# Retention and pooling trunk on one core: PSUM as one pool of eight named banks, GpSimd's first loads held back, the input's first pieces over ScalarE's queue

## Chip, core and metric

One of the eight cores of a Trainium2 chip runs the kernel. The metric is the device time of one launch in microseconds (us); a lower time is better. TensorE is PE, VectorE is DVE, ScalarE is ACT, GpSimd is POOL and SyncE is SP in the rows of the profile.

## What is computed

Two layers over 256 tokens of 2048 numbers in float32, each with a norm before it and a plain residual add, and a last norm.

```
h = x
h = h + (group_norm(retention(rope(q), rope(k), v)) * silu(z)) @ ret_w_out    # q,k,v,z = rms_norm(h) @ ret_w_in, 8 heads
h = h + ((mix @ pool_w_grp + pool_b_grp) * pool_scale * silu(z)) @ pool_w_out # u,z = rms_norm(h) @ pool_w_in
out = rms_norm(h, final_norm)                                                 # mix = windowed mean of u, minus u
```

The weights are 236 units of 128 x 2048 float32 numbers (1024 KB each), plus the first four of `ret_w_in`, which come in pieces. Nearly all the arithmetic is products of these weights with 256 columns of activations.

## The kernel before

**Exactness.** Products run in the fast float32 form of TensorE, which keeps fewer bits of an operand. So each operand is split in two: `hi` is a rounded copy (a CAST on ScalarE, line 91) and `lo` is what is left (a subtraction on VectorE, line 92). A product is then hi x hi, hi x lo and lo x hi. For every weight unit SyncE loads `raw` (line 103, three buffers), ScalarE and VectorE split it in two halves `w` (five buffers), and TensorE multiplies.

**Stages.** (1) The startup (lines 188 to 245): nine products of ones (`cold`), then the input `xin` and the first four units arrive in pieces, each is split, and TensorE accumulates four results `accs`. GpSimd loads the identity `idt`, the rotation table `rp` and two masks `mk` at once. (2) Eight heads of retention (lines 249 to 353): q, k, v and gate products, scores, normalisation. Products that keep the weights stationary are written to `acc` by `stationary` (lines 122 and 123), those of v to `accv` (lines 302 to 304). (3) The way out, `way_out` with `ret_out` (lines 387 to 479): two passes, each of 12 plain units ("C") and 4 mixed units ("S", in which sums of blocks save products); all eight PSUM banks hold running sums `p1`, `p5`, `p6`, `p7`, `c11`, `c12`, `c21`, `c22` (line 363). When the sums of a half are ready, `turn` transposes the new stream on TensorE into `turned` (line 510) and splits it into `hs2`. (4) Pooling (lines 551 to 598): four groups of 8 + 8 units and 4 units of group weights, again by `stationary` into `acc`. (5) `way_out` with `pool_out`, with the last norm in it, and the output.

**Order.** The program text gives an order, and a scheduler that plays the program against its own timing model moves instructions on each engine's queue; each engine then runs its queue strictly in order. A tile may be written when its buffer is free, that is when the last reader of the tile that held it before is done.

**PSUM.** A partition has eight banks of 512 float32 numbers. Stages 1 and 2, and again stage 4, open two pools: three buffers for `acc`, five for the rest (`banks`, lines 80 to 86). Stages 3 and 5 each open a pool of their own with eight tags (lines 492 and 639). The pools of one stage are closed before those of the next are opened on the same memory.

The lines that the change touches: 78 to 86 (`banks`), 138, 188, 196, 197, 241, 256, 272, 292, 320, 341, 557, 578 and 587 (where a bank is taken), 358 (`Sum`), 387 and 399 (`way_out`), 204 (the input's pieces), 223 to 226 (GpSimd's loads), 491 to 520 and 638 to 645 (opening and closing).

Of the kernel before, what the change touches and what calls it, by code (L numbers as in the profile page):

```python
# [7 lines left out]
F32 = mybir.dt.float32  # L8
# [5 lines left out]
P = 128  # L14
D = 2048
S = 256
# [15 lines left out]
FIRST = (20, 16)  # L32

# [12 lines left out]
def kernel(  # L46
# [25 lines left out]
    nc = tc.nc  # L72
# [61 lines left out]
    def column_sums(sums):  # L134

        sp = ev.tile([P, 2, S], F32R, tag="sp", name="sp", bufs=1)
        split(sp[:, 0], sp[:, 1], sums)
        tot = psum[1].tile([P, 512], F32, tag="ret", name="tot")
# [45 lines left out]


    with banks("first"), tc.tile_pool(name="rt", bufs=1) as rt:

        cold = psum[1].tile([P, 512], F32, tag="ret", name="cold")
# [7 lines left out]
        accs = [psum[0].tile([P, 512], F32, tag="acc", name="acc") for _ in range(3)]  # L196
        accs.append(psum[1].tile([P, 512], F32, tag="ret", name="acc"))
# [43 lines left out]
        rst = psum[1].tile([P, 512], F32, tag="ret", name="rst")  # L241
# [7 lines left out]
        for h in range(NH):  # L249
# [3 lines left out]
            for c in range(4 if h else 0):  # L253
                blocks = blocks_of(weights(ret_in[unit]))
                unit += 1
                acc = psum[0].tile([P, 512], F32, tag="acc", name="acc")
                stationary(acc, blocks, hs)
                joined(qk[:, c], acc)
# [13 lines left out]
            sc = psum[1].tile([P, 2, S], F32, tag="ret", name="sc")  # L272
# [19 lines left out]
            accv = [psum[0].tile([P, 512], F32, tag="acc", name="accv") for _ in range(2)]  # L292
# [25 lines left out]
            for c in range(4):  # L318
                cs = slice(c * P, (c + 1) * P)
                po = psum[1].tile([P, 512], F32, tag="ret", name="po")  # L320
# [17 lines left out]
            for c in range(4):  # L338
                blocks = blocks_of(weights(ret_in[unit]))
                unit += 1  # L340
                acc = psum[0].tile([P, 512], F32, tag="acc", name="acc")
# [13 lines left out]
    class Sum:  # L355


        def __init__(self, pool, name, n):
            self.tile, self.n, self.done = pool.tile([P, 512], F32, tag=name, name=name), n, 0
# [27 lines left out]
    def way_out(A, src, first, forms, tmp, pool, work, order, y, after, ends=False):  # L387
# [8 lines left out]
        for p in range(2):  # L396
            plain = len(CLASSIC) // 2 * 12
            sums = {}
            for name in order:
                n = 0 if name == "c22" else 3 * NS  # L400
                sums[name] = Sum(pool, name, n + (plain if name[0] == "c" else 0))
# [79 lines left out]
    with tc.tile_pool(name="pl", bufs=1) as pl:  # L481
# [9 lines left out]
        with (  # L491
            tc.tile_pool(name="way1", bufs=1, space=bass.MemoryType.PSUM) as way,
            tc.tile_pool(name="work1", bufs=1) as work,
        ):
# [4 lines left out]
            def turn(t, c):  # L499
# [5 lines left out]
                for i in range(2):  # L505
                    turned = way.tile([P, 512], F32, tag=(("p1", "p5"), ("p6", "p7"))[c % 2][i], name="turned")
# [10 lines left out]
            order = ("p1", "p5", "p6", "p7", "c11", "c21", "c12", "c22")  # L517
            way_out(os, ret_out, FIRST[0], forms, tmp, way, work, order, stream, turn)
        second = ctx.enter_context(ExitStack())
        second.enter_context(banks("second"))  # L520
# [30 lines left out]
        for g, win in enumerate(WINDOWS):  # L551
# [3 lines left out]
            for c in range(GT):  # L555
                blocks = blocks_of(weights(pool_in[2 * GT * g + c]))
                acc = psum[0].tile([P, 512], F32, tag="acc", name="acc")
# [18 lines left out]
            for c in range(GT):  # L576
                blocks = blocks_of(weights(pool_in[2 * GT * g + GT + c]))
                acc = psum[0].tile([P, 512], F32, tag="acc", name="acc")
# [4 lines left out]
            for c in range(GT // 2):  # L583
                halves = weights(pool_grp[GT // 2 * g + c])
                for i in range(2):
                    e = GT * g + 2 * c + i
                    acc = psum[0].tile([P, 512], F32, tag="acc", name="acc")
# [50 lines left out]
        with (  # L638
            tc.tile_pool(name="way2", bufs=1, space=bass.MemoryType.PSUM) as way,
            tc.tile_pool(name="work2", bufs=1) as work,  # L640
        ):
            tmp = act.tile([P, 4 * S + 2 * P + 512], F32, tag="hs", name="tmp")
            forms = pl.tile([P, NS, 4, 2, P], F32R, tag="ms", name="forms")
            order = ("p1", "p5", "p6", "c11", "c21", "c12", "c22", "p7")
            way_out(gs, pool_out, FIRST[1], forms, tmp, way, work, order, stream, norm, True)

# [110 lines left out]
```

## Time and profile before

| | |
|---|---|
| median of 3 runs | 1393.86 us (1393.78 to 1394.25) |
| the profiled execution | 1391.64 us |
| its span | 1389.5 us |
| TensorE busy | 1364.1 us (98%) |
| VectorE, ScalarE, GpSimd busy | 1060.9 us (76%), 719.7 us (52%), 25.4 us (2%) |
| mean DMA rate | 189 GB/s |

The span is what the profiler saw between the first and the last instruction; the execution's own time lies 2.1 us above it. Matmuls are pipelined, so a row of TensorE shows each one longer than the step from one to the next. The granted clock of TensorE is given as a share of full speed: 1.00 is 2.4 GHz, 0.50 is 1.2 GHz.

### The profile page before, as it was taken

Reading aid. Unit: us, or ns where it says so; the run is one execution under the profiler, and the core shown is the slowest. Engines: PE = TensorE matmul, PEld = TensorE weight load, DVE = VectorE, ACT = ScalarE, POOL = GpSimd, SP = SyncE. Lnnn points to the kernel's source line nnn. Section 1 sums busy time; section 2 is a strip of 40 time slices with the busy share of each in tenths; the row PEclk is TensorE's granted clock in tenths of the full one; section 3 lists DMA queues with packets and bytes.
Section 4 is the critical chain, followed back from the end, with each engine's and each line's share of the span. In section 5 each row is a group of like instructions: output and inputs, shape, how many; then the busy total and the mean of one; then the engine's idle time right before and its main releaser. Section 6 shows DMA issues by size and latency. Waiting matters only on the chain.

```text
span 1389.5 us, 18380 instructions
## 1 busy us (share of the span) xinstructions
PE 1364.1 (98%) x7176; PEld 1171.6 (84%) x7176; DVE 1060.9 (76%) x1545; ACT 719.7 (52%) x1027; POOL 25.4 (2%) x33
## 2 busy tenths in 40 slices
PE   8999999999999999999998999999999999899997
PEld 7888888888888888888887888888888888788885
DVE  6886868686868686898777867876886896868676
ACT  6455545455545454555454455455545545545443
POOL 0000000000000000000000000000000000000102
PEclk8999999999999999999999999999999999999999
DMA  8545454545555545475555555555555555446552
GB/s 298 209 161 197 172 191 177 190 179 188 182 187 180 184 173 190 153 261 196 182 189 180 195 199 182 185 199 195 183 188 191 198 185 185 179 164 230 182 210 93
DMA packets 39493, 262.66 MB, mean 189 GB/s; under 512 B 4512, under 2 KB 4896, under 8 KB 9072
## 3 DMA queue, kind: packets, MB, share of 16 engines
q1 hardware_dynamic: 37872, 255.93, 52.0%
q0 software_dynamic: 1536, 5.57, 1.1%
q8 instruction: 56, 0.92, 0.3%
q14 instruction: 29, 0.24, 0.0%
HBM read 259.39 MB, written 2.10 MB: 188 GB/s over the span
## 4 chain that ended last, share of the span: by engine, by line
PE 96%; DVE 2%; ACT 1%; issue 1%; DMA 1%; SPq 0%; DVEq 0%; ACTq 0%
PE acc L122 37%; PE c L363 21%; PE acc L123 19%; PE accv L302 4%; PE accv L304 4%; PE accv L303 4%; PE p L363 3%; PE po L322 1%; DVE w L92 1%; DMA xin<-in_xT 1%; PE po L324 1%; PE sc L276 0%; DVE hs L97 0%; PE sc L281 0%; ACT w L91 0%
## 5 line engine op out<-in xcount | busy, mean ns | idle before, releaser
L92 DVE TENSOR_TENSOR w<-raw,w 128x1024 fp32r<-128x1024 f32 x472 | 568.1, 1209 | 168.0 <-ACT w L91 160.0
L122 PE MATMUL acc<-hs,w 128*128 128x512 f32 x1984 | 692.4, 392 | 3.5 <-DVE rs_t L161 3.5
L91 ACT CAST w<-raw 128x1024 fp32r<-128x1024 f32 x472 | 486.9, 1038 | 305.0 <-PE acc L123 130.7
L123 PE MATMUL acc<-hs,w 128*128 128x256 f32 x1984 | 556.1, 280 | 0.0
L122 PEld LDWEIGHTS acc<-hs,w 128*128 128x128 f32 x1984 | 372.0, 187 | 84.7 <-issue 3.7
L123 PEld LDWEIGHTS acc<-hs,w 128*128 128x128 f32 x1984 | 375.5, 189 | 1.0
L363 PE MATMUL c<-w,gs 128*128 128x512 f32 x624 | 149.3, 394 | 4.6 <-DVE m L592 4.6
L131 ACT COPY hl<-acc 128x256 f32<-128x256 f32 x128 | 47.9, 374 | 199.5 <-PE acc L123 197.0
L363 PE MATMUL c<-w,os 128*128 128x512 f32 x624 | 149.3, 391 | 0.9 <-DVE gz L132 0.9
L363 PEld LDWEIGHTS c<-w,gs 128*128 128x128 f32 x624 | 118.7, 190 | 30.6 <-issue 4.9
L363 PEld LDWEIGHTS c<-w,os 128*128 128x128 f32 x624 | 116.6, 188 | 26.1 <-DVE gz L132 1.2
L302 PE MATMUL accv<-w,hs 128*128 128x512 f32 x256 | 99.8, 390 | 1.2 <-DVE qk L132 1.2
L303 PE MATMUL accv<-w,hs 128*128 128x512 f32 x256 | 99.8, 390 | 0.0
L304 PE MATMUL accv<-w,hs 128*128 128x512 f32 x256 | 99.7, 390 | 0.0
L122 PE MATMUL acc<-ms,w 128*128 128x512 f32 x256 | 90.6, 397 | 0.0
L123 PE MATMUL acc<-ms,w 128*128 128x256 f32 x256 | 72.0, 281 | 0.0
L91 ACT CAST w<-s 128x1024 fp32r<-128x1024 f32 x32 | 33.6, 1050 | 52.0 <-PE c L363 43.9
L122 PEld LDWEIGHTS acc<-ms,w 128*128 128x128 f32 x256 | 48.1, 188 | 11.8
L92 DVE TENSOR_TENSOR w<-s,w 128x1024 fp32r<-128x1024 f32 x32 | 39.2, 1224 | 24.4 <-ACT w L91 24.4
L302 PEld LDWEIGHTS accv<-w,hs 128*128 128x128 f32 x256 | 48.1, 188 | 11.1 <-DVE qk L132 1.5
L304 PEld LDWEIGHTS accv<-w,hs 128*128 128x128 f32 x256 | 48.0, 188 | 10.1
L303 PEld LDWEIGHTS accv<-w,hs 128*128 128x128 f32 x256 | 48.1, 188 | 9.7
(159 smaller groups left out, 1052.7 us busy)
## 6 DMA issues: line engine op xcount, KB each, us to landing
raw<-in_ret_in SPq DMA_DIRECT2D x92, 1024.0 KB, 4.9
raw<-in_pool_in SPq DMA_DIRECT2D x64, 1024.0 KB, 4.9
raw<-in_ret_out SPq DMA_DIRECT2D x32, 1024.0 KB, 4.9
raw<-in_pool_out SPq DMA_DIRECT2D x32, 1024.0 KB, 4.9
raw<-in_pool_grp SPq DMA_DIRECT2D x16, 1024.0 KB, 4.9
xin<-in_ret_in SPq DMA_DIRECT2D x7, 512.0 KB, 8.5
xn<-in_xN POOLq DMA_DIRECT2D x4, 512.0 KB, 6.9
out<-xn SPq DMA_DIRECT2D x8, 256.0 KB, 2.3
```

Of the source, the lines that this page charges most:

```text
L91: nc.scalar.copy(hi, src)
L92: nc.vector.tensor_tensor(out=lo, in0=src, in1=hi.bitcast(F32), op=ALU.subtract)
L122: nc.tensor.matmul(acc, hi, moving[:, k], start=(k == 0), stop=False)
L123: nc.tensor.matmul(acc[:, :S], lo, moving[:, k, 0], start=False, stop=(k == n - 1))
L131: nc.scalar.copy(t, acc[:, S:])
L302: nc.tensor.matmul(accv[t], hs[:, k, 0, ts], hi[:, ws], start=(k == 0), stop=False)
L303: nc.tensor.matmul(accv[t], hs[:, k, 0, ts], lo[:, ws], start=False, stop=False)
L304: nc.tensor.matmul(accv[t], hs[:, k, 1, ts], hi[:, ws], start=False, stop=(k == KT - 1))
L322: nc.tensor.matmul(po[:, :S], vs[:, 0, p, cs], ss[:, q, :S], start=(n == 0), stop=(n == 2))
L324: nc.tensor.matmul(po[:, S:], vs[:, 1, p, cs], ss[:, :, S:], start=(p == 0), stop=(p == 1))
L363: nc.tensor.matmul(self.tile, a, w, start=(self.done == 0), stop=(self.done == self.n - 1))
```

## The change

All PSUM tiles come from one pool that stays open for the whole program and has eight tags, `b0` to `b7`, one buffer each. `ring("acc")` walks through banks 0 to 2, `ring("ret")` through banks 3 to 7, and both go on counting through the whole program; the sums of `way_out` have fixed banks by their place in `SUMS`, and `turned` takes banks 0, 1 or 2, 7. Besides, a one-element copy on GpSimd that reads `hs[:, 11, 1]` stands ahead of GpSimd's loads, and the first three pieces of the input are issued by ScalarE in place of SyncE. Cut to its core (every other place that took a tile from `psum[0]` or `psum[1]` now calls `ring("acc", ...)` or `ring("ret", ...)` in the same way):

```diff
+SUMS = ("p1", "p5", "p6", "c11", "c21", "c12", "c22", "p7")
...
-    psum = []
-
-    @contextmanager
-    def banks(name):
-
-        with tc.tile_pool(name=f"{name}_acc", bufs=3, space=bass.MemoryType.PSUM) as acc:
-            with tc.tile_pool(name=f"{name}_ret", bufs=5, space=bass.MemoryType.PSUM) as rest:
-                psum[:] = acc, rest
-                yield
+    psum = ctx.enter_context(tc.tile_pool(name="psum", bufs=1, space=bass.MemoryType.PSUM))
+    turns = {"acc": 0, "ret": 0}
+
+    def bank(i, name):
+        return psum.tile([P, 512], F32, tag=f"b{i}", name=name)
+
+    def ring(kind, name):
+
+        start, n = (0, 3) if kind == "acc" else (3, 5)
+        turns[kind] += 1
+        return bank(start + (turns[kind] - 1) % n, name)
...
-                nc.sync.dma_start(out=xin[:, k : k + n], in_=xT[:, k : k + n])
+                queue = nc.scalar if u == 0 else nc.sync
+                queue.dma_start(out=xin[:, k : k + n], in_=xT[:, k : k + n])
                 nc.sync.dma_start(out=raw[:, ws], in_=ret_in[u][:, ws])
...
+        late = rt.tile([P, 1], F32, name="late")
+        tc.keep_in_program_order(nc.gpsimd.tensor_copy(out=late, in_=hs[:, 11, 1, :1].bitcast(F32)))
         idt = const.tile([P, P], F32, name="idt")
         tc.keep_in_program_order(nc.gpsimd.dma_start(out=idt, in_=ident))
...
-            self.tile, self.n, self.done = pool.tile([P, 512], F32, tag=name, name=name), n, 0
+            self.tile, self.n, self.done = bank(i, name), n, 0
...
-                    turned = way.tile([P, 512], F32, tag=(("p1", "p5"), ("p6", "p7"))[c % 2][i], name="turned")
+                    turned = bank(((0, 1), (2, 7))[c % 2][i], "turned")
...
-        second.enter_context(banks("second"))
```

The scheduler makes other queues of the new program. Three places follow. The first is TensorE where pooling (stage 4) begins; `acc` is the result of one weight unit, `turned` a transposed block of the stream, `hs2` the split stream, `c22` a running sum of the stage before. Before:

```order
L363 MATMUL c22_5642<-w_6195,os_357 128x512 x6
L510 MATMUL turned_6228<-idt_303,xn_4987 128x128
L510 MATMUL turned_6237<-idt_303,xn_4987 128x128
L510 MATMUL turned_6228<-idt_303,xn_4987 128x128 x3
L510 MATMUL turned_6237<-idt_303,xn_4987 128x128 x3
L122 MATMUL acc_6280<-hs2_4997,w_6274 128x512
L123 MATMUL acc_6280<-hs2_4997,w_6274 128x256
```

Now, from the last of the running sum to the last transposes:

```order
L370 MATMUL c22_5635<-w_6189,os_356 128x512 x6
L125 MATMUL acc_6267<-hs2_4991,w_6261 128x512
L126 MATMUL acc_6267<-hs2_4991,w_6261 128x256
L125 MATMUL acc_6267<-hs2_4991,w_6261 128x512
L126 MATMUL acc_6267<-hs2_4991,w_6261 128x256
```

```order
L126 MATMUL acc_6267<-hs2_4991,w_6264 128x256
L514 MATMUL turned_6222<-idt_302,xn_4984 128x128 x3
L514 MATMUL turned_6231<-idt_302,xn_4984 128x128 x3
L125 MATMUL acc_6267<-hs2_4991,w_6264 128x512
L126 MATMUL acc_6267<-hs2_4991,w_6264 128x256
L125 MATMUL acc_6395<-hs2_4991,w_6389 128x512
L126 MATMUL acc_6395<-hs2_4991,w_6389 128x256
```

Twenty-two products of the first `acc` now stand ahead of the last six transposes, and behind them come two more and then 24 of another unit's `acc`, before any product that needs the blocks transposed last.

The second place is TensorE at the end of pooling, where `way_out` with `pool_out` begins; `ms` is the split mix, `gs` the split gated result, `c11` and `c21` running sums. Before:

```order
L122 MATMUL acc_10335<-ms_9331,w_10308 128x512
L123 MATMUL acc_10335<-ms_9331,w_10308 128x256
L363 MATMUL c11_10377<-w_10384,gs_6258 128x512 x6
L363 MATMUL c11_10377<-w_10387,gs_6258 128x512 x6
L363 MATMUL c21_10378<-w_10384,gs_6258 128x512 x6
L363 MATMUL c21_10378<-w_10387,gs_6258 128x512 x6
L363 MATMUL c12_10379<-w_10416,gs_6258 128x512 x6
```

Now:

```order
L125 MATMUL acc_10266<-ms_9318,w_10239 128x512
L126 MATMUL acc_10266<-ms_9318,w_10239 128x256
L370 MATMUL c11_10359<-w_10366,gs_6245 128x512
L370 MATMUL c21_10360<-w_10366,gs_6245 128x512
L370 MATMUL c11_10359<-w_10366,gs_6245 128x512 x5
L370 MATMUL c21_10360<-w_10366,gs_6245 128x512 x2
L125 MATMUL acc_10298<-ms_9318,w_10292 128x512
L126 MATMUL acc_10298<-ms_9318,w_10292 128x256
```

Nine products of the last stage now stand ahead of the last two `acc` of pooling; the others follow these two.

The third place is the head of ScalarE's queue; `hs` is the split input, `w` a split weight half. Before:

```order
L182 ACT_TABLE_LOAD
L182 CAST ones<-ones_f 128x128
L96 ACTIVATE hs<-xin,vec 128x256
L91 CAST w<-xin 128x512
...
L96 ACTIVATE hs<-xin,vec 128x256 x2
L232 ACTIVATE xin<-xin 128x1024
L91 CAST w<-xin 128x1024
```

Now:

```order
L208 DMA xin<-in_xT 128x256
L185 ACT_TABLE_LOAD
L185 CAST ones<-ones_f 128x128
L208 DMA xin<-in_xT 128x256
L208 DMA xin<-in_xT 128x512
L99 ACTIVATE hs<-xin,vec 128x256
L94 CAST w<-xin 128x512
...
L99 ACTIVATE hs<-xin,vec 128x256 x2
L94 CAST w<-xin 128x1024
L239 ACTIVATE xin<-xin 128x1024
```

Three issues of the input are new there, two of them behind the table load, and the square of the first input blocks (line 232, now 239) has moved behind the cast of the third piece of weights. In both lists the second pair of `hs` and `w` rows, equal to the first, is left out.

## Rows read from the trace of the kernel before

**Rows 1.** The page, busy time of TensorE and its weight loads.
```profile
PE 1364.1 (98%) x7176; PEld 1171.6 (84%) x7176; DVE 1060.9 (76%) x1545; ACT 719.7 (52%) x1027; POOL 25.4 (2%) x33
```

**Rows 2.** Waits of TensorE: us in total, times, longest.
```profile
PE c L363 <- DVE m L592: 4.6, 1, 4.6
PE acc L221 <- ACT w L91: 4.1, 3, 2.2
PE acc L122 <- DVE rs_t L161: 3.5, 1, 3.5
PE accv L302 <- DVE qk L132: 1.2, 1, 1.2
...
PE c L363 <- DVE gz L132: 0.9, 1, 0.9
PE turned L510 <- DVE xn L408: 0.6, 1, 0.6
```

**Rows 3.** VectorE in order of time (start, length), beside two of these waits.
```profile
755.07 0.48 DVE L97 SCALAR_TENSOR_TENSOR hs<-turned,vec,hs 128x256 fp32r<-128x256 f32 x1
...
1206.92 0.48 DVE L592 SCALAR_TENSOR_TENSOR m<-acc,vec,hl 128x256 f32<-128x256 f32 x1
```

**Rows 4.** Windows after two waits; before the comma PE's busy time, third last its clock.
```profile
755.20:758.50 3.30, 2.81 (x9) 2.45 (x10) 2.52 (x13) 0.41 (x1) 0.00 (x0) 0.50 0.39 164
1205.60:1212.50 6.90, 4.95 (x12) 3.92 (x13) 6.90 (x14) 1.66 (x5) 0.54 (x1) 0.51 0.52 188
```

**Rows 5.** TensorE in order of time after two waits: start, length, idle before.
```profile
755.69 0.77 PE L122 MATMUL acc<-hs,w 128*128 128x512 f32 x1 [3.46 <-DVE rs_t L161]
...
758.39 0.47 PE L122 MATMUL acc<-hs,w 128*128 128x512 f32 x1
...
1207.55 5.03 PE L363 MATMUL c<-w,gs 128*128 128x512 f32 x11 [4.64 <-DVE m L592]
```

**Rows 6.** Groups of TensorE from 1215 to 1225 us: busy time, mean ns.
```profile
L363 PE MATMUL c<-w,gs 128*128 128x512 f32 x46 | 10.6, 389 | 0.0
```

**Rows 7.** ScalarE in order of time, startup.
```profile
0.72 1.28 ACT L182 ACT_TABLE_LOAD   x1 [0.72 <-PEq L746]
...
6.30 0.62 ACT L91 CAST w<-xin 128x512 fp32r<-128x512 f32 x1 [2.34 <-DMA xin<-in_ret_in]
...
12.15 1.06 ACT L232 ACTIVATE xin<-xin 128x1024 f32<-128x1024 f32 x1 [0.55 <-DVE hs L97]
13.12 1.03 ACT L91 CAST w<-xin 128x1024 fp32r<-128x1024 f32 x1
```

**Rows 8.** GpSimd in order of time, its first issues.
```profile
1.28 0.74 POOL L224 DMA_DIRECT2D idt<-in_ident  x1 [0.35 <-issue]
...
2.55 1.06 POOL L271 DMA_DIRECT2D mk<-in_masks  x2
```

**Rows 9.** Windows of the startup: busy PE, PEld, DVE, ACT, POOL, clock, DMA share, GB/s.
```profile
3.00:5.00 2.00, 1.77 (x11) 1.58 (x9) 0.48 (x1) 0.51 (x1) 0.61 (x2) 1.00 0.67 144
...
7.00:9.00 2.00, 2.00 (x8) 1.71 (x8) 1.13 (x2) 0.51 (x1) 0.00 (x0) 0.65 0.99 309
...
11.00:13.00 2.00, 2.00 (x7) 1.63 (x7) 1.08 (x3) 1.45 (x3) 0.00 (x0) 0.50 1.04 413
```

**Rows 10.** The page, DMA issues: KB each, median us to landing.
```profile
mk<-in_masks POOLq DMA_DIRECT2D x8, 192.0 KB, 4.3
...
rp<-in_rope POOLq DMA_DIRECT2D x1, 256.0 KB, 5.9
...
idt<-in_ident POOLq DMA_DIRECT2D x1, 64.0 KB, 4.0
```

**Rows 11.** VectorE in order of time, the first reader of a late load.
```profile
56.54 0.69 DVE L240 TENSOR_TENSOR rpr<-rp,rs 128x512 f32<-128x512 f32 x1
```

**Rows 12.** Windows, columns as in rows 9: startup, first way out.
```profile
20.00:25.00 5.00, 5.00 (x30) 4.36 (x29) 4.47 (x8) 5.00 (x9) 0.00 (x0) 1.00 1.04 419
590.00:600.00 10.00, 10.00 (x46) 8.29 (x45) 10.00 (x14) 4.21 (x7) 2.85 (x4) 1.00 0.88 304
```

More of the change, by code (lines that the diff above doesn't have):

```diff
@@ L1 @@
[L1 removed]
+from contextlib import ExitStack
 import concourse.bass as bass
@@ L183 @@
     hs = act.tile([P, KT, 2, S], F32R, tag="hs", name="hs")
-    with banks("first"), tc.tile_pool(name="rt", bufs=1) as rt:
-        cold = psum[1].tile([P, 512], F32, tag="ret", name="cold")
+    with tc.tile_pool(name="rt", bufs=1) as rt:
+        cold = ring("ret", "cold")
         for _ in range(9):
@@ L195 @@
         qk = rt.tile([P, 4, S], F32, tag="qk", name="qk")
-        accs = [psum[0].tile([P, 512], F32, tag="acc", name="acc") for _ in range(3)]
-        accs.append(psum[1].tile([P, 512], F32, tag="ret", name="acc"))
+        accs = [ring("acc", "acc") for _ in range(3)]
+        accs.append(ring("ret", "acc"))
         for u in range(4):
@@ L240 @@
         nc.vector.tensor_tensor(out=rpr, in0=rp, in1=wide(rs, 2), op=ALU.mult)
-        rst = psum[1].tile([P, 512], F32, tag="ret", name="rst")
+        rst = ring("ret", "rst")
         rsn = rt.tile([P, 2], F32, name="rsn")
@@ L255 @@
                 unit += 1
-                acc = psum[0].tile([P, 512], F32, tag="acc", name="acc")
+                acc = ring("acc", "acc")
                 stationary(acc, blocks, hs)
@@ L289 @@
             split(ss[:, 0], ss[:, 1], sm)
-            accv = [psum[0].tile([P, 512], F32, tag="acc", name="accv") for _ in range(2)]
+            accv = [ring("acc", "accv") for _ in range(2)]
             for c in range(4):
@@ L319 @@
                 cs = slice(c * P, (c + 1) * P)
-                po = psum[1].tile([P, 512], F32, tag="ret", name="po")
+                po = ring("ret", "po")
                 for n, (p, q) in enumerate(((0, 0), (0, 1), (1, 0))):
@@ L340 @@
                 unit += 1
-                acc = psum[0].tile([P, 512], F32, tag="acc", name="acc")
+                acc = ring("acc", "acc")
                 stationary(acc, blocks, hs)
@@ L385, in sides, with way_out @@
         put(3, s)
-    def way_out(A, src, first, forms, tmp, pool, work, order, y, after, ends=False):
+    def way_out(A, src, first, forms, tmp, work, y, after, ends=False):
         def blk(k, t):
@@ L398, in way_out @@
             sums = {}
-            for name in order:
+            for i, name in enumerate(SUMS):
                 n = 0 if name == "c22" else 3 * NS
-                sums[name] = Sum(pool, name, n + (plain if name[0] == "c" else 0))
+                sums[name] = Sum(i, name, n + (plain if name[0] == "c" else 0))
             out_of = {(t, c): sums[f"c{t + 1}{c + 1}"] for t in range(2) for c in range(2)}
@@ L489, in stream @@
             return xn[:, :, cs] if t is None else xn[:, t, cs]
[L491 to L494, printed above, removed]
+        with tc.tile_pool(name="work1", bufs=1) as work:
             tmp = pl.tile([P, 4 * S + 2 * P + 512], F32, tag="gz", name="tmp")
@@ L556 @@
                 blocks = blocks_of(weights(pool_in[2 * GT * g + c]))
-                acc = psum[0].tile([P, 512], F32, tag="acc", name="acc")
+                acc = ring("acc", "acc")
                 stationary(acc, blocks, hs2)
@@ L577 @@
                 blocks = blocks_of(weights(pool_in[2 * GT * g + GT + c]))
-                acc = psum[0].tile([P, 512], F32, tag="acc", name="acc")
+                acc = ring("acc", "acc")
                 stationary(acc, blocks, hs2)
@@ L586 @@
                     e = GT * g + 2 * c + i
-                    acc = psum[0].tile([P, 512], F32, tag="acc", name="acc")
+                    acc = ring("acc", "acc")
                     stationary(acc, blocks_of(halves[i : i + 1]), ms)
@@ L636, in norm @@
                 nc.sync.dma_start(out=out[t][:, ps], in_=piece)
[L638 to L641, printed above, removed]
+        with tc.tile_pool(name="work2", bufs=1) as work:
             tmp = act.tile([P, 4 * S + 2 * P + 512], F32, tag="hs", name="tmp")
             forms = pl.tile([P, NS, 4, 2, P], F32R, tag="ms", name="forms")
-            order = ("p1", "p5", "p6", "c11", "c21", "c12", "c22", "p7")
-            way_out(gs, pool_out, FIRST[1], forms, tmp, way, work, order, stream, norm, True)
+            way_out(gs, pool_out, FIRST[1], forms, tmp, work, stream, norm, True)
 def _layout(inputs):
```

10 lines of the change are left out of this document (4 added, 6 removed).

## Prediction

> **What bounds the kernel now.** I read the page first: TensorE is busy 98% of the span [rows 1], so a change can gain only in the 2% in which it stands, or where it runs at the lower clock. Next came TensorE's own waits, few enough to list [rows 2]. The reader is to see that nearly all are single events: 4.6 us at the first product of the last stage (`c` on `m`), 3.5 us at the first `acc` of pooling, 0.9 us at the first product of the first way out (`c` on `gz`), 0.6 us at a transpose, and in the startup 4.1 us on ScalarE's casts and 1.2 us at the first `accv`.
>
> The question is whether the three at the stage borders wait for data or for a bank. At 1207 us the product needs `gs` blocks of the first groups, finished long ago; what it waits for is `m`, the last reader of an `acc`, at 1206.92 us [rows 3]. At 577 us it is likewise `gz`, a reader of `acc`. At 755 us it is the last split of `turned`, which ends at 755.07 + 0.48 = 755.55 us [rows 3], 0.14 us before TensorE starts at 755.69 us [rows 5] (the row names a tiny instruction of the same engine, which came last by the profile), although the first product reads the block of `hs2` that was split first. So all three wait for a pool to be given back. After two of them the granted clock is 0.50 and 0.51, that is 1.2 GHz, for 3.3 and 6.9 us [rows 4]; it fell while TensorE stood and rose again when TensorE had worked for some us.
>
> **The change part by part.** *One pool of banks.* It adds and removes no instruction of TensorE; a first write now waits for the last reader of its own bank alone. First products of a way out go to `c11` and `c21`, banks 3 and 4, which `acc` never uses, so the waits on `m` and `gz` have nothing left to stand for. The first `acc` of pooling is the 80th tile of a ring of three (3 + 28 + 16 + 32 were taken before), bank 1; the blocks transposed last lie in banks 2 and 7. The new queue of TensorE uses this: 22 products stand ahead of the last transposes and 26 behind them, before the first that needs a late block.
>
> What each border costs, at full pace. A 512-column product takes 10.6 / 46 = 0.23 us from one to the next [rows 6], a pair of `stationary` (512 and 256 columns) one and a half of that, 0.345 us.
> - 1207 us: 4.6 us of waiting; then 11 products took 5.03 us [rows 5] where 11 x 0.23 = 2.53 would do, so 2.5 us of low clock: 7.1 us.
> - 755 us: 3.5 and 0.6 us of waiting; four pairs took 758.39 - 755.69 = 2.70 us [rows 5] for 4 x 0.345 = 1.38, so 1.3 us: 5.4 us.
> - 577 us: 0.9 us.
> - Waits are counted from the shown end of a matmul, which lies 0.39 - 0.23 = 0.16 us behind its slot [rows 6]; for four waits 0.6 us.
>
> Sum 14.0 us. The cover that replaces it at 755 us is 48 products, 24 pairs of 0.345 us, 8.3 us, against 4.1 us of waiting. What could be late next is VectorE, below.
>
> *GpSimd's loads.* Until now 64 + 256 + 2 x 192 = 704 KB [rows 10] are issued from 1.28 to 3.6 us [rows 8], among the first pieces. Now they wait for the split of block 11 of 16. Nothing is queued behind them on GpSimd that is wanted early: their first reader is VectorE at 56.54 us [rows 11], and the longest of these loads lands in 5.9 us in the middle [rows 10]; issued at some 18 us they keep over 25 us of cover. They then run beside the first `raw` units; at 413 GB/s [rows 9] 704 KB are 1.7 us, which ScalarE's queue hides as long as it is not waiting for `raw`.
>
> *The input's first pieces on ScalarE's queue.* Three issues leave SyncE, so its first weights are issued sooner by about 0.45 us each; on ScalarE the second and third stand behind a table load of 1.28 us [rows 7], about 0.6 us later than now. Two queues can then hold work for the same DMA engines.
>
> *What the startup gains.* The third weight piece is cast at 13.12 us, behind a square of 1.06 us [rows 7] that has been moved away. By then 1600 KB of input and weights (64 + 128 + 128 + 256 + 256 + 256 + 512) have come beside the 704 KB. From then on VectorE is nearly solid (4.47 of 5 us from 20 to 25 us [rows 12]) and the first `accv` waits for VectorE [rows 2], so that product moves as the third cast moves. Bounds: at best the 1600 KB flow at 413 GB/s from 3 us on, 4.0 us, and the cast starts at 7.1 us: 6.0 us gained. At worst only the 704 KB are saved, 1.7 us, less 0.6 us of later issue: 1.1 us; a loss is excluded, since the bytes ahead are fewer by a third. In the trace the rate is 144 GB/s from 3 to 5 us, 309 from 7 to 9 and 413 from 11 to 13 us, when GpSimd's transfers run out [rows 9]: they seem to cost more than their bytes. TensorE's own waits of the startup, 4.1 us [rows 2], are the nearest row to what an earlier feed can give back at the same clock (0.50 there [rows 9]); I take a little more, 4.3 us, as a denser start may bring 2.4 GHz sooner.
>
> That is the row; a page speaks against it. The Trainium skill, "DMA: Bandwidth & Descriptors", section "Issuing engines are not separate DMA queues", says that transfers of all issuing engines run on the same 16 DMA engines and that another issuer saves only the time to start a transfer. By that rule this part would give the 1.1 to 1.7 us of the worst bound, and the sum 15.4 instead of 18.3 us. No run here has separated the two; the rates of rows 9 lean against it.
>
> **Sum.** 14.0 + 4.3 = 18.3 us off the profiled execution, 1391.64 to 1373.3 us. The median of the runs lies 2.2 us above that execution; the forecast on its scale is 1393.86 - 18.3 = 1375.6 us.
>
> **The rivals.** *Bytes only.* GpSimd's loads cost the others no more than their own bytes, or ScalarE's late second piece eats the rest. Borders 14.0 plus 1.4: 1378.5 us. For it: the rate of 309 GB/s from 7 to 9 us, with both streams under way, is three quarters of the best. Against it: 144 GB/s before that.
>
> *A border comes back as a wait for VectorE.* From 1205.6 to 1212.5 us VectorE is busy 6.9 of 6.9 us [rows 4] while TensorE stands or crawls: it works off a debt there. Without the pause TensorE arrives sooner and may have to wait for split weights. Five buffers of `w` hold about 5 x 2.8 = 14 us of products (12 products of 0.23 us each half), which speaks against it. If half of the borders' 14 us is given back: 1393.86 - 7.0 - 4.3 = 1382.6 us.
>
> *VectorE becomes the bound of the ways out: slower.* In the first way out it is busy 10.00 of 10 us from 590 to 600 us [rows 12] and TensorE just does not wait. If TensorE, now earlier by 0.9 us at its door, runs into VectorE at every mixed unit, each costs one VectorE instruction of 1.2 us and half-speed products after it as at 755 us, 1.3 us: 16 mixed units x 2.5 = 40 us, 1393.86 - 18.3 + 40 = 1415.6 us. It decides once the lag at a mixed unit exceeds what the five buffers hold; slower than now needs 8 such units. The `w` buffers and the plain units between speak against it.
>
> *The pools already gave single banks back.* Then the borders stay and only the startup counts: 1389.6 us. The wait for the very last reader in rows 2 and 3 speaks against it, and so does the new queue.
>
> **How the numbers follow.** Forecast 0.74; bytes only 0.13; VectorE's debt 0.09; pools already free 0.01; slower 0.03. About 0.2% (2.8 us) is what a measurement of this kernel can tell from no change. The forecast, bytes only and VectorE's debt are all faster by more than that, 0.96 together; 0.01 of them and the rival of the pools, which lies near the edge, go to no change. So faster 0.95, same 0.02, slower 0.03. The forecast's own range runs from 1393.86 - 14.0 - 6.0 = 1373.9 us, less 0.9 us for rounding in the waits, 1373.0, to 1378; with bytes only it reaches to 1380.5 us, and 0.13 is left out above.
>
> **What the profile after would show.** Right: TensorE's waits on `m`, on the last split of `turned` and on `gz` are gone, and no window of 0.50 stands near 740 and 1190 us; the first weight cast of 1024 columns starts between 7 and 9.5 us instead of 13.12; the first `accv` starts near 32.5 us; GpSimd's first issue stands near 18 us. Wrong: a wait of TensorE on `w` in a way out; a third cast later than 11 us; or a low clock right through the startup with the first `accv` after 34 us.

## The result and the profile after

The kernel after takes **1379.84 us** in the median of 4 runs (1378.45 to 1380.32), the kernel before 1394.05 us on the same chip (4 runs, 1393.78 to 1394.55): 0.9896 times as long, 95% interval 0.9879 to 0.9913. That is 14.2 us less; the forecast said 18.3. The time lies 4.2 us above the forecast's 1375.6 us: over the range that the prediction gave the forecast itself (1373.0 to 1378 us), and inside the wider one that takes in *bytes only* (to 1380.5 us).

The page, the busy time of the engines in the kernel after (it answers to [rows 1]):

```profile
PE 1363.1 (99%) x7176; PEld 1168.4 (85%) x7176; DVE 1059.1 (77%) x1545; ACT 718.5 (52%) x1027; POOL 26.5 (2%) x34
```

TensorE's waits in the kernel after (us in total, times, longest), all of them; they answer to [rows 2]:

```profile
PE accv L309 <- DVE qk L135: 2.9, 1, 2.9
PE acc L225 <- ACT w L94: 1.2, 1, 1.2
PE cold L193 <- POOL ones_f L183: 1.0, 1, 1.0
```

The waits on `m`, on the last split of `turned` and on `gz` are gone. In exchange the wait at the first `accv` has grown from 1.2 to 2.9 us. The windows of the early feed, at the three borders and around the first `accv`, kernel after (busy time of PE, PEld, DVE, ACT, POOL, then PE's granted clock, DMA share, GB/s), answer to [rows 4] and, the first, to [rows 9]:

```profile
3.00:5.00 2.00, 2.00 (x11) 1.89 (x9) 0.48 (x1) 0.51 (x1) 0.00 (x0) 1.00 0.77 160
...
570.00:580.00 10.00, 10.00 (x56) 8.59 (x55) 7.69 (x14) 4.88 (x9) 0.00 (x0) 1.00 0.48 158
748.00:756.00 8.00, 8.00 (x48) 6.95 (x47) 5.87 (x13) 5.32 (x10) 0.00 (x0) 1.00 0.50 178
1190.00:1200.00 10.00, 10.00 (x56) 8.59 (x55) 8.40 (x15) 5.00 (x9) 0.00 (x0) 1.00 0.38 136
30.70:33.80 3.10, 0.25 (x3) 0.01 (x1) 3.10 (x5) 1.07 (x2) 0.00 (x0) 1.00 0.91 307
33.80:37.30 3.50, 3.50 (x8) 2.79 (x9) 3.03 (x7) 1.09 (x3) 0.00 (x0) 0.51 0.83 309
```

At the borders TensorE is busy throughout at 1.00. The two low windows of [rows 4] have no successor there, but a new one stands behind the first `accv`: TensorE stands for 3.1 us, and then eight products take 3.5 us where 8 x 0.23 = 1.8 would do.

ScalarE's start in order of time, kernel after (rows ending in ACTq are issues; it answers to [rows 7]):

```profile
0.72 0.41 ACTq L208 DMA_DIRECT2D xin<-in_xT  x1
1.16 1.28 ACT L185 ACT_TABLE_LOAD   x1 [1.16 <-PEq L744]
1.22 0.87 ACTq L208 DMA_DIRECT2D xin<-in_xT  x2
...
9.63 1.03 ACT L94 CAST w<-xin 128x1024 fp32r<-128x1024 f32 x1
10.57 1.06 ACT L239 ACTIVATE xin<-xin 128x1024 f32<-128x1024 f32 x1
```

The third weight cast starts at 9.63 instead of 13.12 us.

**Where the time went.** TensorE works through the same products in both kernels, so the start of the same product (the n-th that writes a tile of that name) can be set side by side. Both columns are starts in the two profiled executions, in us; the last one is how far the kernel after is ahead (minus) or behind.

| product | before | after | after - before | gained since the row above |
|---|---|---|---|---|
| first `accv`, first head | 36.94 | 33.80 | -3.14 | 3.1 |
| first `accv`, second head | 107.90 | 106.37 | -1.53 | -1.6 (low clock) |
| last `tot` of the last head | 574.58 | 575.20 | +0.62 | -2.15 (seven heads) |
| first `c`, first way out | 577.64 | 577.17 | -0.46 | 1.1 (border) |
| a `c` late in that stage | 738.70 | 738.13 | -0.57 | 0.1 |
| an `acc` of the first pooling group | 801.58 | 795.39 | -6.19 | 5.6 (border) |
| an `acc` behind the second group | 975.08 | 970.18 | -4.90 | -1.3 |
| a `c` early in the last stage | 1212.67 | 1200.62 | -12.05 | 7.15 (border) |
| last `c` | 1379.54 | 1367.73 | -11.81 | -0.2 |

So the borders gave 13.9 us by this table, against 14.0 forecast; the startup gave 1.5 and not 4.3; and 3.6 us net were lost in stretches without any wait, which no step of the prediction has. The two profiled executions lie 11.3 us apart, where the medians lie 14.2 us apart: that of before is 2.4 us below its median, that of after 0.5 us above. Experiment e10 looks at that.

### The profile page after: what moved, and what is told of

Read it like the earlier page. It is cut to its first block, busy times and chain, and to the rows that moved or that the text cites. A ratio compares the mean times of both kernels' runs of the same rounds, so it can differ in the third digit from the quotient of the medians.

```text
span 1378.2 us, 18382 instructions
## 1 busy us (share of the span) xinstructions
PE 1363.1 (99%) x7176; PEld 1168.4 (85%) x7176; DVE 1059.1 (77%) x1545; ACT 718.5 (52%) x1027; POOL 26.5 (2%) x34
## 4 chain that ended last, share of the span: by engine, by line
PE 97%; ACT 1%; DVE 1%; DMA 0%; issue 0%; SPq 0%; DVEq 0%; ACTq 0%
PE acc L125 38%; PE c L370 21%; PE acc L126 19%; PE accv L309 4%; PE accv L310 4%; PE accv L311 4%; PE p L370 3%; PE po L329 1%; PE po L331 1%; DMA xin<-in_ret_in 0%; ACT w L94 0%; PE sc L283 0%; ACT hs L99 0%; PE sc L288 0%; DVE w L95 0%
```

## Experiments

Ten runs, in three sessions (e1 to e4, e5 to e8, e9 and e10). In each the kernel before ran beside them, with medians of 1393.2, 1393.49 and 1393.07 us; beside the kernel after it had 1394.05 us. So where two kernels of different sessions are compared, up to 1.0 us of the difference can be the session's.

### One part of the change at a time

**e1_pool_only**, the kernel after less these lines (and the pieces of the input on SyncE):

```diff
-        late = rt.tile([P, 1], F32, name="late")
-        tc.keep_in_program_order(nc.gpsimd.tensor_copy(out=late, in_=hs[:, 11, 1, :1].bitcast(F32)))
-                queue = nc.scalar if u == 0 else nc.sync
-                queue.dma_start(out=xin[:, k : k + n], in_=xT[:, k : k + n])
+                nc.sync.dma_start(out=xin[:, k : k + n], in_=xT[:, k : k + n])
```

> The kernel before with the named banks alone: the input's pieces stay on SyncE and GpSimd's loads stay early. Theory 'holes': matched product by product, the two traces differ by 1.1 us at 577 us, 5.8 us at 755 us and 7.2 us at 1207 us, 14.1 in all; the startup gave 1.5 us and some 3.8 us were lost in stretches where TensorE's pairs took 353 instead of 347 ns. Then this kernel takes 1394.05 - 14.1 = 1380 us if the slower pace does not come along, up to 1383.8 us if it does, with the third weight cast near 13.1 us and the first accv near 36.9 us. Rival 'startup as forecast': the startup gave 4.3 us of the 14.2 and the borders only 9.9; then it takes 1384.2 us and a wait of over 1 us stands at a border.

Measured: 1378.72 us (4 runs, 1378.52 to 1379.03), ratio 0.9898 (0.9884 to 0.9912), 14.5 us less than before. No wait stands at a border. The windows there, kernel e1_pool_only:

```profile
750.00:757.00 7.00, 7.00 (x45) 6.17 (x44) 6.51 (x19) 3.91 (x8) 0.00 (x0) 1.00 0.57 180
1195.00:1205.00 10.00, 10.00 (x51) 8.46 (x50) 8.68 (x17) 6.69 (x12) 0.54 (x1) 1.00 0.53 176
```

The named banks alone bring all of the result: with them alone the kernel is no slower than with the whole change. "Holes" holds, the rival (1384.2 us) falls. The banks and the new order that the scheduler makes from them come together here; no run has the one without the other.

**e2_start_only**, the kernel before with the added lines of the diff above.

> The kernel before with its two nested pools kept, but GpSimd's loads held back and the input's first pieces on ScalarE's queue. Theory 'holes': the startup gives 3.1 us at the first accv, half of it lost again to a low clock behind the longer wait there: 1.5 us, so 1392.5 us, or up to 1395 us if a slower pace comes along; all three border waits (4.6, 3.5, 0.9 us) are back. Rival 'startup as forecast': 4.3 us, 1389.7 us.

Measured: 1394.78 us (11 runs, 1393.1 to 1397.0), ratio 1.0012 (1.0003 to 1.0021): **1.6 us slower** than before. The border waits are back, and with them the new one. The first of TensorE's waits, kernel e2_start_only (that on `gz`, 0.9 us, is further down):

```profile
PE c L366 <- DVE m L595: 4.6, 1, 4.6
PE acc L122 <- DVE rs_t L161: 3.5, 1, 3.5
PE accv L305 <- DVE qk L132: 2.9, 1, 2.9
```

Its first `accv` starts at 34.16 us, 2.8 us earlier than before, and yet the whole is slower. So the two startup edits together are a loss. Which of them?

**e3_no_scalar_queue**, the kernel after with the input's first pieces on SyncE (second half of e1's edit).

> The kernel after with all pieces of the input on SyncE again; GpSimd's loads stay late, and every engine's order but the issues is the same. Theory 'issue only': the second queue saves only SyncE's time for three issues, so the third weight cast moves from 9.6 us to 10.0-11.0 us and the whole by 0.4 to 1.4 us, 1380.2 to 1381.2 us. Rival 'two queues feed faster': the third cast goes back to 12 us or later and the whole loses 2.4 us or more, 1382.2 us. Rival 'no use': the third cast is no later than 9.6 us, and the time stays at 1379.8 us.

Measured: 1379.89 us (4 runs, 1378.87 to 1380.64) in the session of e1, against 1379.84 for the kernel after in its own: no difference. ScalarE's start, kernel e3_no_scalar_queue:

```profile
4.82 0.62 ACT L94 CAST w<-xin 128x512 fp32r<-128x512 f32 x1 [0.83 <-DMA xin<-in_ret_in]
...
9.84 1.04 ACT L94 CAST w<-xin 128x1024 fp32r<-128x1024 f32 x1 [1.05 <-DMA xin<-in_ret_in]
```

With one queue the first weights are cast 0.9 us sooner (4.82 instead of 5.71 us in the kernel after) and the third piece 0.2 us later (9.84 instead of 9.63). "Issue only" had the size of it too large, "no use" is right in the time: with GpSimd's loads held back, the second queue is worth nothing. The rule of the Trainium skill that the prediction set against its own row ("DMA: Bandwidth & Descriptors", section "Issuing engines are not separate DMA queues") agrees with this run.

**e4_no_late**, the kernel after without the holding copy (first half of e1's edit).

> The kernel after without the small copy that holds GpSimd's loads back: 704 KB come among the first pieces again, ScalarE's queue stays. Theory 'bytes only': they cost 704 KB / 413 GB/s = 1.7 us, so the third weight cast starts near 11.3 us and the first accv near 35.5 us; of that the low clock behind the first accv may give back up to 1.6 us: 1379.9 to 1381.5 us. Rival 'more than their bytes' (the prediction's reading): the third cast goes back to 13 us, 1383 us or more.

Measured: **1376.32 us** (4 runs, 1376.08 to 1376.55), ratio 0.9880 (0.9865 to 0.9895): 3.5 us less than the kernel after. Both expectations had the sign wrong. ScalarE's third cast, kernel e4_no_late:

```profile
11.97 1.04 ACT L94 CAST w<-xin 128x1024 fp32r<-128x1024 f32 x1 [0.91 <-DMA xin<-in_ret_in]
```

VectorE in order of time, kernel e4_no_late:

```profile
30.43 2.35 DVE L95 TENSOR_TENSOR w<-raw,w 128x1024 fp32r<-128x1024 f32 x2
32.70 1.22 DVE L239 TENSOR_TENSOR xin<-xin 128x1024 f32<-128x1024 f32 x1
33.83 0.75 DVE L135 TENSOR_TENSOR qk<-acc,hl 128x256 f32<-128x256 f32 x2
```

The same place in the kernel after:

```profile
29.92 1.22 DVE L241 TENSOR_TENSOR xin<-xin 128x1024 f32<-128x1024 f32 x1
31.05 2.35 DVE L95 TENSOR_TENSOR w<-raw,w 128x1024 fp32r<-128x1024 f32 x2
33.32 0.75 DVE L135 TENSOR_TENSOR qk<-acc,hl 128x256 f32<-128x256 f32 x2
```

Holding the loads back does speed the feed, by 2.3 us at the third cast (11.97 to 9.63 us), and VectorE starts the sum of 1024 columns (lines 239 and 241) 2.8 us sooner. But the order of VectorE's queue differs. In the kernel after, two splits of `w` (2.35 us) stand between that sum and the joins (`qk`); in e4_no_late they stand behind the joins. So the joins come only 0.5 us sooner. The first `accv` needs the banks that these joins read. In e4_no_late TensorE gets there at about the time of the joins and does not stand; in the kernel after it gets there 3 us ahead of them, stands, and pays the low clock.

What this order is worth, e1_pool_only shows. It differs from e4_no_late in the queue of the three input pieces alone, and took 2.4 us longer in the same session (1378.72 against 1376.32 us). VectorE in order of time, kernel e1_pool_only:

```profile
32.80 1.22 DVE L238 TENSOR_TENSOR xin<-xin 128x1024 f32<-128x1024 f32 x1
33.93 2.36 DVE L95 TENSOR_TENSOR w<-raw,w 128x1024 fp32r<-128x1024 f32 x2
36.20 0.75 DVE L135 TENSOR_TENSOR qk<-acc,hl 128x256 f32<-128x256 f32 x2
```

The sum starts within 0.1 us of that in e4_no_late, but the two splits stand ahead of the joins here too, and the joins come 2.4 us later; so does the first `accv` (36.68 against 34.30 us). The three issues change the order that the scheduler gives VectorE: without held loads that is worth 2.4 us, and with them (e3_no_scalar_queue and the kernel after) the order is the slow one with either queue. No run changed the order by itself.

Of the lead of e4_no_late over the kernel after 0.73 us stand at the second head's first `accv` (105.64 against 106.37 us); the larger part, 2.2 us, grows by equal steps through the seven heads after it. The kernels that have the holding tile all show these steps, those without it never.

### The tile of four bytes

The tile `late` takes 32 bytes of a partition, and the tiles of the heads that are allocated behind it (`rp`, `qs`, `ss`, `vs`, `gz` and others) all lie 32 bytes higher. Is it the address, or when GpSimd's loads run?

**e5_hold_no_tile**, from the kernel after:

```diff
-        late = rt.tile([P, 1], F32, name="late")
-        tc.keep_in_program_order(nc.gpsimd.tensor_copy(out=late, in_=hs[:, 11, 1, :1].bitcast(F32)))
         idt = const.tile([P, P], F32, name="idt")
+        tc.keep_in_program_order(nc.gpsimd.tensor_copy(out=idt[:, :1], in_=hs[:, 11, 1, :1].bitcast(F32)))
```

> The kernel after, with the holding copy written into the first column of idt (which its load then overwrites) instead of a tile of its own: GpSimd's loads stay as late, every engine's order stays, but the tiles of the heads (qs, ss, vs, gz and others) lie 32 bytes lower, as in the kernel before. Seen so far: matched product by product, the kernels with that tile lose 0.305 us in each of heads 1 to 7 against those without it, 2.1 us in all. Theory 'address': that loss is gone, 1379.84 - 2.1 = 1377.7 us, and the last stages start 2.1 us earlier than in after. Rival 'lateness': it comes from when GpSimd's loads run; then nothing changes, 1379.8 us.

**e6_tile_only**, from e4_no_late:

```diff
+        late = rt.tile([P, 1], F32, name="late")
```

> The kernel after with early GpSimd loads (as e4_no_late), and a tile of 4 bytes that nothing writes or reads, at the place of the one that was left out: orders as in e4_no_late, the heads' tiles 32 bytes higher. Theory 'address': the loss of 0.305 us a head comes back, 1376.3 + 2.1 = 1378.5 us. Rival 'lateness': 1376.3 us.

Measured: e5_hold_no_tile 1377.92 us (4 runs, 1376.05 to 1378.58), e6_tile_only 1378.31 us (4 runs, 1378.28 to 1378.78), where 1377.7 and 1378.5 were expected. The first product of `accv` in the second and in the last head, kernel after:

```profile
106.37 0.39 PE L309 MATMUL accv<-w,hs 128*128 128x512 f32 x1
...
528.93 0.39 PE L309 MATMUL accv<-w,hs 128*128 128x512 f32 x1
```

Kernel e5_hold_no_tile:

```profile
107.11 0.40 PE L308 MATMUL accv<-w,hs 128*128 128x512 f32 x1
...
527.80 0.39 PE L308 MATMUL accv<-w,hs 128*128 128x512 f32 x1
```

Kernel e6_tile_only:

```profile
105.11 0.40 PE L308 MATMUL accv<-w,hs 128*128 128x512 f32 x1
...
527.66 0.39 PE L308 MATMUL accv<-w,hs 128*128 128x512 f32 x1
```

Six heads take 422.56 us with the tile in the kernel after and 422.55 in e6, 420.69 without it in e5, and 107.90 to 528.62, that is 420.72 us, in the kernel before. The address makes it, in both directions: 0.31 us a head. No wait of TensorE shows it. It lies in the pace of `stationary`: behind the products `po`, which read `ss` and `vs`, a pair of products takes 353 instead of 347 ns until the next `tot`. Matched product by product in the third head, the kernel after loses nothing against e5 up to `po`, 0.30 us from there to `tot`, and nothing more up to the next head. Why TensorE keeps the slower step after operands that lie 32 bytes higher stays open.

The same four kernels say what the held loads are worth without the tile. By medians the tile costs 1.9 to 2.0 us (1377.92 to 1379.84 with the loads held, 1376.32 to 1378.31 with early loads), and holding the loads costs another 1.5 to 1.6 us (1376.32 to 1377.92 without the tile, 1378.31 to 1379.84 with it). These compare sessions, but the second head's first `accv` has it too: 105.64 us in e4_no_late and 107.11 in e5_hold_no_tile. So beside ScalarE's queue holding the loads back is a loss by itself. It goes with the order above: e4_no_late and e6_tile_only, with early loads and ScalarE's queue, are the only two kernels that have the joins ahead of the two splits. With SyncE's queue alone, where the order stays, held loads and tile together cost 1.2 us (1378.72 to 1379.89, e1_pool_only to e3_no_scalar_queue), less than the tile; there the held loads gain, by an estimate from these differences, 0.7 to 0.8 us.

**e10_before_again**, the kernel before unchanged.

> The kernel before, profiled once more. Seen so far: its profiled execution took 1391.64 us, its runs 1393.2 to 1394.05 us in the median; and the stretch of pooling from 866 to 956 us ran at 347 ns a pair there, while six other kernels with the same order of products ran it at 353 ns. Theory 'state of the run': which of the two paces a group of pooling gets is a matter of the execution; in this profile one or more groups of pooling run at 353 ns and the execution takes 1393 us or more. Rival 'state of the program': the same program takes the same paces, and this profile shows 347 ns there again, at 1391.6 us or with the difference elsewhere.

Measured: 1392.75 us (10 runs, 1391.95 to 1394.35), its profiled execution 1392.22 us. Two windows of pooling (the count behind PE's busy time is its products), kernel before:

```profile
770.00:840.00 70.00, 70.00 (x405) 61.72 (x404) 52.08 (x79) 34.34 (x51) 0.55 (x1) 1.00 0.56 195
880.00:940.00 60.00, 60.00 (x348) 52.90 (x347) 47.79 (x80) 30.13 (x45) 0.54 (x1) 1.00 0.56 196
```

Kernel e10_before_again:

```profile
770.00:840.00 70.00, 70.00 (x398) 60.68 (x397) 50.93 (x78) 33.94 (x50) 0.55 (x1) 1.00 0.56 194
880.00:940.00 60.00, 60.00 (x349) 52.91 (x348) 48.26 (x81) 29.57 (x45) 0.54 (x1) 1.00 0.55 193
```

Kernel after:

```profile
770.00:840.00 70.00, 70.00 (x406) 61.17 (x405) 52.25 (x81) 34.71 (x51) 0.55 (x1) 1.00 0.57 197
880.00:940.00 60.00, 60.00 (x341) 52.08 (x340) 45.43 (x75) 29.50 (x44) 0.54 (x1) 1.00 0.55 194
```

The same program runs the first group of pooling (770 to 840 us) with 405 products in one execution and 398 in the other, at the same granted clock. So the pace there is a matter of the execution, and costs 1.9 us in e10 from 755 to 862 us. In the stretch that the expectation names, 866 to 956 us, e10 runs at 347 ns once more, as the rival has it; it is the first group that shows two paces of one program. The profiled time is 0.8 us under the 1393 us expected.

In the kernel after it is the second group (880 to 940 us) that is slow. The twelve traces together tell whether that is the change's doing. Kernel e6_tile_only:

```profile
770.00:840.00 70.00, 70.00 (x399) 60.67 (x398) 50.97 (x79) 34.21 (x51) 0.55 (x1) 1.00 0.57 197
880.00:940.00 60.00, 60.00 (x348) 52.91 (x348) 46.58 (x75) 29.75 (x44) 0.54 (x1) 1.00 0.57 196
```

The first group is slow in e6, e9 and e10, the second in the kernel after, e1 to e5, e7 and e8, and neither in the first profile of the kernel before. e6 and e9 have the named banks and the pattern of e10; e2_start_only has the pools of before and the pattern of the kernel after. So which group is slow does not follow the banks, and the 1.3 us that the table above shows lost there come from the pair of executions that it sets side by side. The first profile of the kernel before paid in neither group; as an estimate from the 1.9 us in e10, that is the main part of the 2.4 us by which it lies below its median.

A second thing differs between the two executions of the kernel before. At the border of 1207 us the low clock lasted 6.9 us in the first [rows 4] and 3.5 us in e10, where all of this comes 1.2 us later. Kernel e10_before_again:

```profile
1208.80:1212.30 3.50, 3.50 (x9) 2.78 (x10) 3.50 (x7) 1.21 (x3) 0.54 (x1) 0.51 0.28 63
```

Matched product by product, that border costs 0.7 us less in e10.

### The wait that is left

**e7_free_banks**, from e5_hold_no_tile:

```diff
-        accs = [ring("acc", "acc") for _ in range(3)]
-        accs.append(ring("ret", "acc"))
+        accs = [ring("ret", "acc") for _ in range(4)]
```

> The kernel after without the holding tile (as e5_hold_no_tile), and the four sums of the startup all taken from the ring of five banks, so that the first accv finds the banks 0 and 1 empty and waits for no join. Theory 'bank': the hole before the first accv (3.1 us between the starts of two products) and the low clock behind it (1.6 us) are gone: first accv near 31 us, 1377.7 - 4.5 = 1373.2 us. Rival 'VectorE': the products only stand a little later, on a split of w or on the join that the scores need, since VectorE's work is the same; then the time stays within 1 us of e5_hold_no_tile, 1376.7 to 1378.7 us.

Measured: 1376.37 us (4 runs, 1375.68 to 1377.12), 1.55 us less than e5_hold_no_tile. The first `accv` does start at 30.69 instead of 34.20 us, without a wait, but TensorE's waits, kernel e7_free_banks, have a new first row:

```profile
PE rst L249 <- DVE rsn L250: 1.8, 1, 1.8
```

The windows around it, kernel e7_free_banks:

```profile
58.40:60.60 2.20, 0.41 (x4) 0.16 (x2) 2.20 (x4) 1.43 (x3) 0.00 (x0) 1.00 0.70 160
60.50:64.20 3.70, 3.60 (x11) 2.82 (x12) 3.09 (x7) 1.81 (x3) 0.00 (x0) 0.64 0.48 204
```

TensorE runs into VectorE again at the second transpose of the norm, and the low clock follows there. Of 3.5 us 1.5 are left at the second head's first `accv` (105.62 against 107.11 us): the bank was the wait, and VectorE's chain the next one. Neither expected time was met; the rival's mechanism is the nearer one.

**e8_free_banks_gpsimd**, from e7_free_banks:

```diff
-            nc.vector.tensor_tensor(out=xin[:, :n], in0=xin[:, :n], in1=xin[:, n : 2 * n], op=ALU.add)
+            nc.gpsimd.tensor_tensor(out=xin[:, :n], in0=xin[:, :n], in1=xin[:, n : 2 * n], op=ALU.add)
```

> As e7_free_banks, and the three larger sums of the squares (2048, 1024 and 512 columns, 2.29, 1.22 and 0.68 us of VectorE) moved to GpSimd. Theory 'bank': nothing is left to gain at the first accv, so the time is that of e7_free_banks, 1373.2 us, within 0.7 us. Rival 'VectorE': it frees 4.2 us on VectorE ahead of the joins, and takes off what e7_free_banks left of the 4.5 us: 1373 us with e7_free_banks at 1376.7 us or more. A third way: GpSimd's sums are so slow that the normalisation (tot, rst) is late: over 1379 us.

Measured: 1376.74 us (4 runs, 1376.1 to 1377.59), within the spread of e7_free_banks, and none of the three expected times; its own wait of 1.6 us stands at an `acc` whose bank an `accv` still holds. Nothing was freed on VectorE: its joins come at 37.63 us, 4.9 us later than in e7_free_banks. GpSimd in order of time, kernel e8_free_banks_gpsimd:

```profile
25.29 4.62 POOL L239 TENSOR_TENSOR xin<-xin 128x2048 f32<-128x2048 f32 x1 [2.83 <-ACT xin L237]
29.99 3.26 POOL L239 TENSOR_TENSOR xin<-xin 128x1024 f32<-128x1024 f32 x1
```

VectorE beside it, same kernel; the last row stands beside no sum of GpSimd:

```profile
26.17 4.83 DVE L95 TENSOR_TENSOR w<-raw,w 128x1024 fp32r<-128x1024 f32 x1 [0.93 <-ACT w L94]
30.93 3.42 DVE L95 TENSOR_TENSOR w<-raw,w 128x1024 fp32r<-128x1024 f32 x1
...
36.49 1.21 DVE L95 TENSOR_TENSOR w<-raw,w 128x1024 fp32r<-128x1024 f32 x1
```

The two engines take turns. A split that starts beside a sum of GpSimd ends 1.1 us after that sum has ended (31.00 after 29.91 us, 34.35 after 33.25), and alone it takes 1.21 us: it stood while the sum ran. The sum of 1024 columns ends 2.25 us after the split ahead of it, about half of the 4.62 us that 2048 columns took: it stood too. The Trainium skill, "SBUF — State Buffer", section "Who interferes with whom", says that a VectorE instruction with two inputs in SBUF contends with a GpSimd instruction that reads SBUF; the trace agrees.

**e9_spare_bank**, from e7_free_banks, takes the two waits away that e7 and e8 ran into:

```diff
         accs = [ring("ret", "acc") for _ in range(4)]
+        spare = ring("ret", "accv")
...
             nc.tensor.transpose(rst[:, t * P : (t + 1) * P], rs[:, t * P : (t + 1) * P], idt)
+        for t in range(2):
             nc.vector.tensor_copy(rsn[:, t : t + 1], rst[:, t * P : t * P + 1])
...
-            accv = [ring("acc", "accv") for _ in range(2)]
+            accv = [ring("acc", "accv"), ring("acc", "accv") if h else spare]
```

> As e7_free_banks, with two more edits at what it ran into: both transposes of rst stand ahead of the two copies that read them, so the second no longer waits for VectorE, and the second accv of the first head takes a spare bank of the ring of five, so that the next two acc find empty banks and not that of an accv which ScalarE has yet to read. Theory 'bank': e7_free_banks moved its gain of 3.5 us into a hole of 2.1 us at 58.4 us and a low clock behind it; without that the gain holds: 1376.4 - 3.0 = 1373.4 us, with no wait of TensorE over 1 us after the startup's weight casts. Rival 'VectorE': the debt is only moved on once more, to the scores or the first po, and the time stays between 1375.4 and 1377 us.

Measured: **1373.25 us** (4 runs, 1372.95 to 1373.4), ratio 0.9858 (0.9841 to 0.9874), with 1373.4 expected. TensorE's waits, kernel e9_spare_bank, all of them:

```profile
PE acc L225 <- ACT w L94: 1.9, 1, 1.9
PE cold L193 <- POOL ones_f L183: 1.0, 1, 1.0
```

The windows where the others stood, kernel e9_spare_bank:

```profile
30.00:40.00 10.00, 10.00 (x47) 8.30 (x46) 9.07 (x12) 5.21 (x8) 0.00 (x0) 1.00 0.80 272
58.00:65.00 7.00, 7.00 (x42) 6.04 (x42) 7.00 (x13) 4.53 (x7) 0.00 (x0) 1.00 0.42 150
```

Theory "bank" holds, the rival (1375.4 to 1377 us) falls; which of the two added edits brings how much was not separated. This version beats both kernels: by medians it is 6.6 us under the kernel after, 5.6 if each is taken against the kernel before of its own session. Here the earlier start is kept: the first `accv` of the second head starts at 101.99 us, 5.9 us ahead of the kernel before.

## Why the prediction was right, and where it was not

- **The three borders, 14.0 us: right.** They gave 13.9 us in the table of equal products: 1.1 for 0.9, 5.6 for 5.4, 7.15 for 7.1, the rest of the 14.0 being the 0.6 us of matmul ends. Reading a wait on a late reader of another bank as a wait for the pool was right; e1_pool_only gives 14.5 us by medians. The cover of 48 products at 755 us sufficed. That sum and table agree to 0.1 us is in part luck: both are read from the same execution of the kernel before, and in e10 the border at 1207 us costs 0.7 us less.
- **"These loads keep over 25 us of cover": right.** No engine waits for `idt`, `rp` or `mk` in the kernel after.
- **"On ScalarE the second and third stand behind a table load": wrong.** They are issued from 1.22 us on, while the table load runs from 1.16 to 2.44 us; the issues went on. Beside held loads it changed nothing, as e3_no_scalar_queue shows; beside early loads these issues were worth 2.4 us, by the order of VectorE and not by the transfers (e1_pool_only against e4_no_late).
- **"They seem to cost more than their bytes": hardly.** Holding 704 KB back brought the third cast forward by 2.3 us against e4_no_late (11.97 to 9.63 us) and by 1.8 us against e6_tile_only (11.46 us), near the 1.7 us of the bytes at 413 GB/s and far from the 4.3 us that were taken. The rate of 144 GB/s from 3 to 5 us [rows 9], on which the larger figure leant, does not tell. With SyncE's queue alone it is 238 GB/s once the loads are held, with ScalarE's queue 145 GB/s (e4_no_late) and 160 (kernel after). Kernel e3_no_scalar_queue:

```profile
3.00:5.00 2.00, 2.00 (x11) 1.89 (x9) 0.48 (x1) 0.69 (x2) 0.00 (x0) 1.00 0.71 238
```

- **"That product moves as the third cast moves", and so 4.3 us from the startup: this is the step that failed.** The cast moved 3.5 us (part of it by the square that went behind it). TensorE's last product ahead of the first `accv` moved 4.8 us (35.48 to 30.67 us), but VectorE's joins, and with them the first `accv`, only 3.1 us, and 1.6 us of that went again at 1.2 GHz behind a wait that had grown from 1.2 to 2.9 us. The prediction saw that VectorE sets that product, and that TensorE's clock falls when it stands; it did not put the two together: a feed that gets TensorE to VectorE's wait sooner lengthens the wait, and the wait has its price behind it. Net 1.5 us for 4.3, where executions with the startup of before scatter by 0.7 us (first `accv` at 36.94, 36.68 and 36.28 us). Nor did it ask what stands ahead of the joins in VectorE's queue: e4_no_late has them ahead of two splits, and with a third cast 2.3 us later it still reaches the second head 0.73 us before the kernel after.
- **A term that was missing: the holding tile moves the heads' tiles by 32 bytes.** 2.15 us, shown both ways by e5_hold_no_tile and e6_tile_only. "A loss is excluded" was wrong with it: the startup edits together lose 1.6 us (e2_start_only).
- **How near the time came is in part luck.** The banks alone bring 14.5 us (e1_pool_only), so of the 4.3 us for the startup nothing is left in the medians; its 1.5 us and the 2.15 us of the tile, which the prediction did not have, cancel. Of its signs, the waits at the borders went as said; the third cast (9.63 us for 7 to 9.5), the first `accv` (33.80 for 32.5) and GpSimd's first issue (20.98 for 18) all came a little late.
- **The rivals.** *Bytes only* (1378.5 us) names the time nearest to the result, and its rule on queues agrees with e3_no_scalar_queue, but not all that is missing was lost in the feed: the cast moved 3.5 us. *A border comes back as a wait for VectorE* and *VectorE becomes the bound of the ways out* did not happen: the list of waits has no entry after 34 us. *The pools already gave single banks back* falls with e1_pool_only.

## What to carry to other kernels

A wait of TensorE at a stage border that ends with the last reader of another bank is a wait for the pool, and one set of named banks for the whole program takes it away together with the low clock behind it: the sum of both, read from the trace, was 14.0 us, and 13.9 (equal products) to 14.5 us (medians) came. An earlier feed is worth only what the next wait leaves of it: follow the product that is to move up to the engine that sets it, and free that one's bank or chain too. An edit of a few issues can make the scheduler order another engine's queue anew (VectorE's joins here, 2.4 us): compare the queues before the edit itself is given the gain or the loss. A tile added to a pool moves all that lie behind it; where a kernel is 99% TensorE, compare the same product in both traces stage by stage, since a pace that is 2% slower shows in no list of waits.

## What the runs showed of the hardware

- TensorE has two paces for the same stream of 512- and 256-column products at the granted clock of 1.00, 347 and 353 ns a pair. In the heads the slower one follows the operands' address (32 bytes; 70.4 instead of 70.1 us a head in each trace with the holding tile, and in none without it). In pooling it differs between executions of one program (405 and 398 products in the same 70 us), and eleven of the twelve traces have exactly one of the first two groups at 353 ns. What switches it was not found.
- Adds on GpSimd and splits on VectorE, each with two inputs in SBUF, took turns: splits of 1.21 us took 4.83 and 3.42 us, and ended 1.1 us after the add beside them.
- ScalarE's queue went on issuing DMAs (from 1.22 us) while its table load ran (1.16 to 2.44 us).
